# Hybrid decoder block, one core: the seven products of the down-projection in another order

## The chip, the cores and the metric

The kernel runs on one core of one Trainium2 chip. A core has TensorE (PE, with its weight loads shown apart as PEld), VectorE (DVE), ScalarE (ACT), GpSimd (POOL) and SyncE (SP), which issues most transfers. The metric is the device time of one execution in microseconds. The profile shows one further execution: its span runs from the first to the last instruction, and its own time is a little longer than its span.

## The reference

One decoder block over 1024 tokens of width 1024: token mixing (sliding-window attention and an mLSTM), cross-attention into 256 memory tokens, a gated MLP, and a last RMSNorm. The change touches only the end of it:

```
u = hf @ w_up[l]
g = causal_depthwise_conv(u[..., :D_FF], conv_ffn_w[l], conv_ffn_b[l])
x = x + (jax.nn.silu(g) * u[..., D_FF:]) @ w_down[l]
return rmsnorm(x, norm_final_g)
```

Here `D_FF` is 2816, so the down-projection multiplies a 1024 x 2816 matrix by a 2816 x 1024 one, in float32. The result, with the residual added, is normalised row by row and multiplied by the gain `norm_final_g`.

## The kernel before, in words

**Precision.** Every float32 operand is split into a rounded high part (a cast on ACT, tiles `dh`) and a remainder (a subtraction on DVE, tiles `dl`). A product is three matmuls: high x high, high x remainder, remainder x high (`three`, line 139).

**Seven products.** Up- and down-projection are done by a scheme of the Strassen kind: each matrix is cut in 2 x 2 blocks, and seven products of block sums, P1 to P7, replace eight block products. The up-projection (tiles `pu`, `w`, `c`, `fu`, `fa`) writes the left-hand blocks and their sums (`A11`, `A12`, `A22`, `S1` to `S4`) to a scratch tensor `pc_d` in DRAM. The down-projection reads them back. It is what the change is about.

**One step.** The inner dimension is worked through in 11 steps (`kp`, 0 to 10). `step` (line 1162) loads one 128 x 1024 tile `dr` by two transfers of 256 KB on SP's queue: the left half from `pc_d`, the right half from the weights. For P5 and P7 it loads a second weight block (`do`, three buffers) and DVE subtracts it from the right half. For P6 and P4 DVE subtracts with a block kept from an earlier product: P6's sum uses P5's, and P4's uses P6's. P1, P2 and P3 use a plain weight block. I call this subtraction the block difference (`drP<-drP,doP` or `drP<-drP,drP` in the profile). Then ACT casts the tile (`dhP<-drP`) and DVE makes the remainder (`dlP<-drP,dhP`). High parts and remainders live in a ring of six buffers, that is three steps; a cast has to wait until the matmuls of three steps before are done. For the last product they stay in larger buffers for steps 0 to 7, since they are read twice.

**PE.** A step of a product is 12 matmuls of 128 x 512: four blocks of 128 rows (i = 0 to 3, one PSUM bank `pdP` each), three matmuls each. So a product is 132 matmuls. The last product is done in two halves: rows 0 and 1 over all steps (6 matmuls a step), then row 2 over all steps, then row 3, so that rows finish one after the other.

**The order around the change.** The products come P1, P2, P5, P6, P3, P7, P4. What follows a product, adding its four results into the residual rows `x2n` (8 tiles of 128 x 1024, rows 0 to 3 and 4 to 7), is put into a list (`later`) and worked off during the steps of the next product (`work`). A scheduler sets the final order of each engine's instructions in most of this; the part at the end is pinned to the written order. Each engine, and SP's queue, works its instructions off in order.

**The end of a row.** When a half row is done, ACT squares it and sums the squares (`half_done`, line 1227, tiles `sq`, `ms`). For the half that is done first POOL multiplies it by the gain (tile `ot`). When both halves are there, POOL adds the two sums and takes the power -0.5 (`root`, line 1237); I call the chain from the last addition over square, sum and power the root chain. Then (`finish`, line 1242) DVE multiplies the late half by root and gain, ACT scales the early half by the root, and two transfers of 256 KB store the row (line 1250), all on SP's queue but one of the very last row, which ACT issues. Rows 0 to 3 end with P3 (fifth product), rows 4 to 7 with P4 (last).

Of the kernel before, what the change touches and what calls it, by code (L numbers as in the profile page):

```python
# [10 lines left out]
AF = mybir.ActivationFunctionType  # L11
ALU = mybir.AluOpType
# [6 lines left out]
D = 1024  # L19
KT = D // P  # L20
NB = S // P
# [4 lines left out]
EPS = 1e-6  # L26
# [7 lines left out]
NK = NFF // 2  # L34
# [25 lines left out]
def kernel(  # L60
# [5 lines left out]
    nc = tc.nc  # L66
    V, A, G, T = [Pinned(tc, e) for e in (nc.vector, nc.scalar, nc.gpsimd, nc.tensor)]
# [8 lines left out]
    def slot(name, dt=F32, pool=None):  # L76
        return (pool or big).tile([P, SLOT], dt, tag="t", name=name)

    def full(name, dt=F32, pool=None):
        return slot(name, dt, pool)[:, :S]  # L80

    def ps_mm(name):
        return mm.tile([P, HALF], F32, tag="mm", name=name)
# [49 lines left out]
    def w_cols(w, c0, n, k0=0, kn=KT):  # L133

        src = w[k0 * P:(k0 + kn) * P, c0:c0 + n].rearrange("(k p) c -> p k c", p=P)
        hi, lo = load_w([(lambda t: t.rearrange("p (k c) -> p k c", k=kn), src)], kn * n)
        return [t[:, :kn * n].rearrange("p (k c) -> p k c", k=kn) for t in (hi, lo)]
# [188 lines left out]
    with ExitStack() as actx:  # L326
# [75 lines left out]
        for h in range(MH):  # L402
            qk = []
            for s_ in range(2):
# [13 lines left out]
                for d in (1, 2, 3):  # L418
                    V.scalar_tensor_tensor(acc[:, d:], u[:, :S - d], col(C_QK + (3 - d) * 8 + ci), acc[:, d:],
                                           op0=ALU.mult, op1=ALU.add)  # L420
# [3 lines left out]
            if h % 2 == 0:  # L424
# [4 lines left out]
                for which, base in ((0, 1792), (1, 2304)):  # L429
                    if h == 0 and which == 0:  # L430
                        continue
                    parts = [w_cols(win, base + h * P, 2 * P, k0=kk, kn=4) for kk in (0, 4)]
                    for i in range(NB):
                        ps = ps_mm(f"pvo{h}_{which}_{i}")
# [25 lines left out]
            for hf in range(2):  # L460
                psc = ps_sm(f"psc{h}_{hf}")
                for ci in range(4):
# [5 lines left out]
                                       op0=ALU.mult, op1=ALU.mult)  # L468
# [5 lines left out]
                for ci in range(4):  # L474
                    c = hf * 4 + ci
                    A.activation(kt[:, ci * P:(ci + 1) * P], pkt[:, ci * P:(ci + 1) * P], AF.Copy,
                                 scale=W[:, c, P - 1:P])
                pht = ps_sm(f"pht{h}_{hf}")
                for ci in range(4):
# [7 lines left out]
                    if c < NB - 1:  # L487
# [3 lines left out]
                        if c:  # L491
                            V.scalar_tensor_tensor(Cn, C, wbc[:, (c + 1) * P - 1:(c + 1) * P], pu,
                                                   op0=ALU.mult, op1=ALU.add)
# [139 lines left out]
    for i in range(2):  # L633
        t = full(f"mn{i}", pool=ep)
        nc.sync.dma_start(t, mem[0][i * P:(i + 1) * P, :])
        sq = full(f"msq{i}", pool=ep)
# [49 lines left out]
    late = []  # L686
    for ct in range(KT):
# [16 lines left out]
        if ct < 5 or ct == KT - 1:  # L704
            hx += [split_gain(t, f"hx{c}", col(G_X + c)) for c, t in late]
            late = []
# [104 lines left out]
    cp = ctx.enter_context(tc.tile_pool(name="cp", bufs=8, reuse_waits="tile"))  # L811
# [169 lines left out]
    for hf in range(2):  # L981
        sl = slice(hf * HALF, (hf + 1) * HALF)
        sqf = full(f"sqf{hf}")[:, :HALF]
        for k in range(4):
# [4 lines left out]
            for q in range(2):  # L989
# [7 lines left out]
                ps = ps_mm(f"pyx{hf}_{ct}")  # L997
# [149 lines left out]
    xr_ = []  # L1147
# [3 lines left out]
    gfb = full("gfb")  # L1151
    nc.sync.dma_start(gfb, norm_final_g.partition_broadcast(P))
    cols = [slice(0, HALF), slice(HALF, S)]
# [4 lines left out]
    def rows(kp, odd, h):  # L1158
        k = 2 * kp + odd
        return wdn[k * P:(k + 1) * P, cols[h]]  # L1160

    def step(name, piece, kp):

        raw = full(f"dr{name}_{kp}")
        b = raw[:, HALF:S]
        nc.sync.dma_start(raw[:, 0:HALF], pc_d[kp, PIECE[piece]])
        odd, h = {"P1": (0, 0), "P2": (1, 0), "P5": (0, 1), "P6": (1, 1), "P3": (1, 1), "P7": (1, 1), "P4": (1, 0)}[name]
        nc.sync.dma_start(b, rows(kp, odd, h))
        if name in ("P5", "P7"):
            other = wpool.tile([P, WSLOT], F32, tag="raw", name=f"do{name}_{kp}")[:, 0:HALF]  # L1170
            nc.sync.dma_start(other, rows(kp, 0, 1 if name == "P7" else 0))
            V.tensor_tensor(b, b, other, op=ALU.subtract)
        if name == "P6":
            V.tensor_tensor(b, b, kept[kp], op=ALU.subtract)
        if name == "P4":
            V.tensor_tensor(b, kept[kp], b, op=ALU.subtract)
        if name in ("P5", "P6"):
            kept[kp] = b
        ring = not (name == "P4" and kp < NK - 3 or name == "P1" and kp < 3)
        hi, lo = [wpool.tile([P, WSLOT], F32R, tag="ws", name=f"d{q}{name}_{kp}", bufs=6) if ring  # L1180
                  else full(f"d{q}{name}_{kp}", F32R) for q in "hl"]
        A.copy(hi, raw)
        V.tensor_tensor(lo, raw, hi.bitcast(F32), op=ALU.subtract)
        return hi, lo

    def bank(name):
        banks[0] += 1
        return (ps_mm if banks[0] % 8 < 3 else ps_sm)(name)

    def along(ps, i, parts, kp):  # L1190
        hi, lo = parts
        sl = slice(i * P, (i + 1) * P)
        three(ps, hi[:, HALF:S], lo[:, HALF:S], hi[:, sl], lo[:, sl], kp == 0, kp == NK - 1, wstat=False)
# [3 lines left out]
    def work(n):  # L1197

        while todo and n:
            todo.pop(0)()  # L1200
            n -= 1

    def multiply_all(name, piece):
        ps = [bank(f"pd{name}_{i}") for i in range(4)]
        n = -(-len(todo) // (NK - 2))
        for kp in range(NK):
            parts = step(name, piece, kp)
            if name == "P1" and kp == 2:
                ups[-1].end()
            for i in range(4):  # L1210
                along(ps[i], i, parts, kp)
            if kp:
                work(n)
        work(-1)
        return ps

    def later(f, *a):
        todo.append(lambda: f(*a))

    def add(i, h, src, op=ALU.add):  # L1220
        x = xr_[i][:, cols[h]]
        V.tensor_tensor(x, x, src, op=op)


    ots, mss = {}, {}

    def half_done(i, h, early):
        if i not in ots:
            ots[i] = full(f"ot{i}", pool=cp), full(f"sq{i}", pool=cp)
            mss[i] = const.tile([P, 2], F32, name=f"ms{i}", tag="ms", bufs=8)  # L1230
        ot, sq = ots[i]
        A.activation(sq[:, cols[h]], xr_[i][:, cols[h]], AF.Square, scale=D ** -0.5, accum_out=mss[i][:, h:h + 1])
        if early:
            G.tensor_scalar(mss[i][:, h:h + 1], mss[i][:, h:h + 1], EPS, None, op0=ALU.add)
            G.tensor_tensor(ot[:, cols[h]], xr_[i][:, cols[h]], gfb[:, cols[h]], op=ALU.mult)

    def root(i):
        ms = mss[i]
        G.tensor_tensor(ms[:, 0:1], ms[:, 1:2], ms[:, 0:1], op=ALU.add)
        G.tensor_tensor(ms[:, 0:1], ms[:, 0:1], mhalf[:, 0:1], op=ALU.pow)  # L1240

    def finish(i, early):

        ot, r3 = ots[i][0], mss[i][:, 0:1]
        late = 1 - early
        V.scalar_tensor_tensor(ot[:, cols[late]], xr_[i][:, cols[late]], r3, gfb[:, cols[late]],
                               op0=ALU.mult, op1=ALU.mult)
        A.activation(ot[:, cols[early]], ot[:, cols[early]], AF.Copy, scale=r3)
        for h in (late, early):
            (A if h == early and i == NB - 1 else nc.sync).dma_start(  # L1250
                out[0][i * P:(i + 1) * P, cols[h]], ot[:, cols[h]])

    for i, p1 in enumerate(multiply_all("P1", "A11")):
        later(A.copy, U[i], p1)
        later(add, i, 0, p1)
    for i, p2 in enumerate(multiply_all("P2", "A12")):
        later(add, i, 0, p2)
    for i, p5 in enumerate(multiply_all("P5", "S1")):
        later(add, i, 1, p5)
        later(add, 4 + i, 1, p5)  # L1260
    for i, p6 in enumerate(multiply_all("P6", "S2")):
        later(lambda i, p: V.tensor_tensor(U[i], U[i], p, op=ALU.add), i, p6)
        later(add, i, 1, U[i])
    for i in range(4):
        later(add, 4 + i, 1, U[i])
        later(add, 4 + i, 0, U[i])
    for i, p3 in enumerate(multiply_all("P3", "S4")):
        later(add, i, 1, p3)
        later(half_done, i, 0, True)
        later(half_done, i, 1, False)  # L1270
        later(root, i)
        later(finish, i, 0)
    for i, p7 in enumerate(multiply_all("P7", "S3")):
        later(add, 4 + i, 1, p7)
        later(add, 4 + i, 0, p7)
        later(half_done, 4 + i, 1, True)

    parts = []
    ps = [bank(f"pdP4_{i}") for i in range(4)]
    for kp in range(NK):  # L1280
        parts.append(step("P4", "A22", kp))
        for i in range(2):
            along(ps[i], i, parts[kp], kp)
        work(2)
    work(-1)
    Pinned.on = True
    for i in range(4):
        if i > 1:
            for kp in range(NK):
                along(ps[i], i, parts[kp], kp)  # L1290
        add(4 + i, 0, ps[i], ALU.subtract)
        half_done(4 + i, 0, False)
        root(4 + i)
        finish(4 + i, 1)
    Pinned.on = False


# [39 lines left out]
```

## Time and profile before

| | |
|---|---|
| three timed runs, median | 1410.37 us (1408.91 to 1410.59) |
| profiled execution, own time | 1409.79 us |
| its span | 1408.0 us |
| PE, DVE, ACT, POOL busy | 97%, 68%, 43%, 9% of the span |
| mean granted TensorE clock | 0.992 of full speed |
| down-projection, first to last matmul | 1181.08 to 1400.75 us |

In the profile's rows a time is in microseconds from the span's start; a row of the timeline gives start, duration, engine, operation, output and inputs (numbers left out, so that every product's tiles read alike: `pdP`, `dhP`, `dlP`, `drP`), how many it merges, and in brackets how long the engine stood idle before and what ended that. SPq and ACTq are the transfers that SP and ACT issue. PE's duration of one matmul is longer than the distance between two, since they are pipelined.

### The profile page before, as it was taken

The page shows a single profiled execution, that of the slowest core. Times are in us where ns is not written, and L with a number is a line of the kernel's source. Part 1 is how long each engine was busy: PE and PEld are TensorE (multiplying, and loading weights), DVE is VectorE, ACT ScalarE, POOL GpSimd, SP SyncE. Part 2 cuts the span into 40 slices and gives each one's busy share as a digit, 9 for nine tenths or more (in the row PEclk, how much of TensorE's full clock was granted, in tenths as well). Part 3 has the DMA queues.
Part 4 walks back from the last instruction along what each step waited for, and adds up shares of the span by engine and source line. Part 5 has one row for each costly group of instructions (what it writes and reads, how often), then busy time and mean ns, then how long its engine had stood idle before and what let it go on. Part 6 is the DMA issues. An engine that isn't in the chain of part 4 may idle for free.

```text
span 1408.0 us, 18518 instructions
## 1 busy us (share of the span) xinstructions
PE 1371.4 (97%) x6956; PEld 1145.4 (81%) x6956; DVE 963.9 (68%) x1647; ACT 612.1 (43%) x1064; POOL 120.6 (9%) x114
## 2 busy tenths in 40 slices
PE   9999999998999999999998999999999999999997
PEld 8888998776788988888886777888888887888875
DVE  6846616878654634355568888888888886596884
ACT  6264344566643433354443433333333333443453
POOL 0200000001000000000015730000000000020030
PEclk9999999999999999999999999999999999999999
DMA  5321132000244531116350123333333348695751
GB/s 179 94 76 60 31 91 61 22 25 22 92 153 152 178 95 31 30 46 189 111 172 8 30 98 112 112 113 112 99 99 109 113 157 299 234 327 187 232 208 60
DMA packets 168138, 162.59 MB, mean 115 GB/s; under 512 B 16296, under 2 KB 122920, under 8 KB 168048
## 3 DMA queue, kind: packets, MB, share of 16 engines
q1 hardware_dynamic: 166096, 155.03, 33.7%
q10 hardware_dynamic: 1440, 4.54, 0.9%
q0 software_dynamic: 512, 1.84, 0.3%
q8 instruction: 55, 0.90, 0.3%
q14 instruction: 35, 0.29, 0.1%
HBM read 128.57 MB, written 32.80 MB: 115 GB/s over the span
## 4 chain that ended last, share of the span: by engine, by line
PE 81%; DVE 10%; DMA 3%; POOL 2%; issue 2%; ACT 2%; SPq 0%; POOLq 0%; DVEq 0%; ACTq 0%
PE pu_T L50 12%; PE pdP L50 11%; PE pu_B L50 9%; PE pyx L50 6%; PE pmq L50 6%; PE pqx L50 6%; PE py L50 6%; PE pvo L50 4%; PE pvg L50 3%; PE pq L50 2%; PE pkx L50 2%; PE psx L50 2%; PE pox L50 2%; PE pvx L50 2%; PE po L50 2%
## 5 line engine op out<-in xcount | busy, mean ns | idle before, releaser
L50 PE MATMUL pu_T<-T,w_T 128*128 128x512 f32 x1056 | 253.0, 395 | 8.9 <-DVE T L50 2.4
L50 PEld LDWEIGHTS pu_T<-T,w_T 128*128 128x128 f32 x1056 | 200.5, 190 | 55.0 <-DVE T L50 3.4
L50 PE MATMUL pu_B<-B,w_B 128*128 128x512 f32 x792 | 188.7, 392 | 3.3 <-DVE w_B L50 3.0
L50 PEld LDWEIGHTS pu_B<-B,w_B 128*128 128x128 f32 x792 | 149.1, 189 | 35.4 <-DVE w_B L50 3.7
L50 DVE TENSOR_TENSOR wlo<-raw,whi 128x1024 fp32r<-128x1024 f32 x67 | 82.3, 1230 | 91.8 <-ACT whi L50 91.2
L50 PE MATMUL pdP<-dlP,dhP 128*128 128x512 f32 x308 | 121.0, 393 | 5.3 <-DVE dlP L50 5.2
L50 ACT CAST dhP<-drP 128x1024 fp32r<-128x1024 f32 x77 | 80.1, 1052 | 105.4 <-PE pdP L50 73.2
L50 ACT CAST whi<-raw 128x1024 fp32r<-128x1024 f32 x67 | 70.3, 1053 | 122.1 <-PE pqx L50 28.4
L50 DVE TENSOR_TENSOR dlP<-drP,dhP 128x1024 fp32r<-128x1024 f32 x77 | 94.8, 1238 | 37.5 <-ACT dhP L50 35.6
L50 PE MATMUL pdP<-dhP,dlP 128*128 128x512 f32 x308 | 120.0, 390 | 0.0
L50 PE MATMUL pdP<-dhP 128*128 128x512 f32 x308 | 118.4, 391 | 1.6 <-ACT dhP L50 1.6
L50 ACT CAST w_T<-s 128x512 fp32r<-128x512 f32 x66 | 40.6, 621 | 96.1 <-PE pu_T L50 54.5
L50 PEld LDWEIGHTS pdP<-dlP,dhP 128*128 128x128 f32 x308 | 57.8, 188 | 20.9 <-DVE dlP L50 9.3
L50 PEld LDWEIGHTS pdP<-dhP 128*128 128x128 f32 x308 | 57.5, 188 | 14.9 <-ACT dhP L50 3.0
L50 PEld LDWEIGHTS pdP<-dhP,dlP 128*128 128x128 f32 x308 | 57.8, 188 | 11.7
L50 DVE SCALAR_TENSOR_TENSOR fa<-fu,vec,fa 128x1023 f32<-128x1023 f32 (+1 forms) x44 | 58.6, 1331 | 2.7 <-ACT fa L50 2.7
L50 DVE TENSOR_TENSOR c<-pu_T,c 128x512 f32<-128x512 f32 x88 | 58.0, 681 | 0.1
L50 PE MATMUL pvo<-whi,hh 128*128 128x256 f32 x192 | 54.7, 285 | 1.1 <-ACT sg L50 1.1
L50 PE MATMUL pvo<-wlo,hh 128*128 128x256 f32 x192 | 54.4, 283 | 0.0
L50 PE MATMUL pvo<-whi,hl 128*128 128x256 f32 x192 | 54.4, 283 | 0.0
L50 PE MATMUL pmq<-hh,whi 128*128 128x512 f32 x128 | 51.6, 403 | 0.0
L50 PE MATMUL pmq<-hh,wlo 128*128 128x512 f32 x128 | 51.1, 399 | 0.0
(463 smaller groups left out, 3034.9 us busy)
## 6 DMA issues: line engine op xcount, KB each, us to landing
c<-in_w_up_dram SPq DMA_DIRECT2D x44, 512.0 KB, 3.8
drP<-pc_d SPq DMA_DIRECT2D x77, 256.0 KB, 5.1
drP<-in_w_down_dram SPq DMA_DIRECT2D x77, 256.0 KB, 5.2
pc_d<-fa SPq DMA_DIRECT2D x20, 512.0 KB, 3.9
raw<-in_wkv_x_dram SPq DMA_DIRECT2D x16, 512.0 KB, 4.0
raw<-in_wo_x_dram SPq DMA_DIRECT2D x16, 512.0 KB, 3.7
raw<-in_w_in_dram SPq DMA_DIRECT2D x15, 512.0 KB, 3.6
doP<-in_w_down_dram SPq DMA_DIRECT2D x22, 256.0 KB, 4.6
```

The source lines that it names most:

```text
L50: ins = f(*a, **k)
```

## The change

The products come P1, P5, P6, P2, P7, P4, P3. The last one is now P3, whose weight block is plain: its steps have no block difference. Rows 4 to 7 now end with the sixth product (P4), and rows 0 to 3 with the last one (P3). The last product's steps are issued four ahead of their matmuls. The gain of an early half is multiplied on DVE in place (`gained_half`) where POOL did it into a second tile; the tiles `ot` and `sq` go, and the squares are written to one tile `junk`. Rows 4 to 7 are stored from ACT's queue, both halves; rows 0 to 3 as the last rows were before: from SP's queue, but for one half of the last row.

```
-        ring = not (name == "P4" and kp < NK - 3 or name == "P1" and kp < 3)
+        ring = not (name == "P3" and kp < NK - 3 or name == "P1" and kp < 3)
...
-    ots, mss = {}, {}
-
-    def half_done(i, h, early):
-        if i not in ots:
-            ots[i] = full(f"ot{i}", pool=cp), full(f"sq{i}", pool=cp)
+    junk, mss = full("junk", pool=cp), {}
+
+    def half_done(i, h):
+        if i not in mss:
...
-        if early:
-            G.tensor_scalar(mss[i][:, h:h + 1], mss[i][:, h:h + 1], EPS, None, op0=ALU.add)
-            G.tensor_tensor(ot[:, cols[h]], xr_[i][:, cols[h]], gfb[:, cols[h]], op=ALU.mult)
+    def gained_half(i, h):
+
+        G.tensor_scalar(mss[i][:, h:h + 1], mss[i][:, h:h + 1], EPS, None, op0=ALU.add)
+        V.tensor_tensor(xr_[i][:, cols[h]], xr_[i][:, cols[h]], gfb[:, cols[h]], op=ALU.mult)
...
         for h in (late, early):
-            (A if h == early and i == NB - 1 else nc.sync).dma_start(
+            (A if i > 3 or h == early and i == 3 else nc.sync).dma_start(
...
-    for i, p2 in enumerate(multiply_all("P2", "A12")):
-        later(add, i, 0, p2)
     for i, p5 in enumerate(multiply_all("P5", "S1")):
...
-    for i, p3 in enumerate(multiply_all("P3", "S4")):
-        later(add, i, 1, p3)
-        later(half_done, i, 0, True)
-        later(half_done, i, 1, False)
-        later(root, i)
-        later(finish, i, 0)
+    for i, p2 in enumerate(multiply_all("P2", "A12")):
+        later(add, i, 0, p2)
+        later(half_done, i, 0)
+        later(gained_half, i, 0)
     for i, p7 in enumerate(multiply_all("P7", "S3")):
         later(add, 4 + i, 1, p7)
         later(add, 4 + i, 0, p7)
-        later(half_done, 4 + i, 1, True)
+        later(half_done, 4 + i, 1)
+        later(gained_half, 4 + i, 1)
+    for i, p4 in enumerate(multiply_all("P4", "A22")):
+        later(add, 4 + i, 0, p4, ALU.subtract)
+        later(half_done, 4 + i, 0)
+        later(root, 4 + i)
+        later(finish, 4 + i, 1)
...
-    ps = [bank(f"pdP4_{i}") for i in range(4)]
+    ps = [bank(f"pdP3_{i}") for i in range(4)]
     for kp in range(NK):
-        parts.append(step("P4", "A22", kp))
+        while len(parts) < min(kp + 4, NK):
+            parts.append(step("P3", "S4", len(parts)))
         for i in range(2):
             along(ps[i], i, parts[kp], kp)
...
-        add(4 + i, 0, ps[i], ALU.subtract)
-        half_done(4 + i, 0, False)
-        root(4 + i)
-        finish(4 + i, 1)
+        add(i, 1, ps[i])
+        half_done(i, 1)
+        root(i)
+        finish(i, 0)
```

DVE's order in the first half of the last product, before. `P4_5` is step 5 of P4; a tile `dr` on the left of the arrow is a block difference, `dl` a remainder, `x2n7` row 7 of the residual:

```order
L50 TENSOR_TENSOR x2n7_9997<-x2n7_9997,pdP7_3_11166 128x512 x2
L50 TENSOR_TENSOR dlP4_4_11548<-drP4_4_11543,dhP4_4_11547 128x1024
L50 TENSOR_TENSOR drP4_5_11564<-drP6_5_10810,drP4_5_11564 128x512
L50 TENSOR_TENSOR dlP4_5_11569<-drP4_5_11564,dhP4_5_11568 128x1024
L50 TENSOR_TENSOR drP4_6_11585<-drP6_6_10831,drP4_6_11585 128x512
L50 TENSOR_TENSOR dlP4_6_11590<-drP4_6_11585,dhP4_6_11589 128x1024
L50 TENSOR_TENSOR drP4_7_11599<-drP6_7_10852,drP4_7_11599 128x512
L50 TENSOR_TENSOR dlP4_7_11604<-drP4_7_11599,dhP4_7_11603 128x1024
```

DVE's order at the same place, now (the last product is P3, and rows 4 to 7 end here):

```order
L50 TENSOR_TENSOR dlP3_5_11524<-drP3_5_11520,dhP3_5_11523 128x1024
L50 TENSOR_TENSOR x2n4_9991<-x2n4_9991,pdP4_0_11213 128x512
L50 TENSOR_TENSOR x2n5_9993<-x2n5_9993,pdP4_1_11214 128x512
L50 TENSOR_TENSOR x2n6_9995<-x2n6_9995,pdP4_2_11215 128x512
L50 SCALAR_TENSOR_TENSOR x2n4_9991<-x2n4_9991,ms4_11279,gfb_9999 128x512
L50 TENSOR_TENSOR dlP3_6_11539<-drP3_6_11535,dhP3_6_11538 128x1024
L50 TENSOR_TENSOR x2n7_9997<-x2n7_9997,pdP4_3_11216 128x512
L50 SCALAR_TENSOR_TENSOR x2n5_9993<-x2n5_9993,ms5_11325,gfb_9999 128x512
L50 SCALAR_TENSOR_TENSOR x2n6_9995<-x2n6_9995,ms6_11371,gfb_9999 128x512
L50 TENSOR_TENSOR dlP3_7_11558<-drP3_7_11554,dhP3_7_11557 128x1024
L50 SCALAR_TENSOR_TENSOR x2n7_9997<-x2n7_9997,ms7_11417,gfb_9999 128x512
L50 TENSOR_TENSOR dlP3_8_11573<-drP3_8_11569,dhP3_8_11572 128x1024
```

Before, block difference and remainder alternate. Now no block difference stands here; the remainders of steps 0 to 5 stand before the sixth product's results, and those of steps 6 to 8 between the ends of rows 4 to 7.

ACT's order at the same place, before (casts `dh`, squares `sq`):

```order
L50 ACTIVATE sq6_11558,ms6_11559<-x2n6_9995 128x512
L50 CAST dhP4_4_11547<-drP4_4_11543 128x1024
L50 ACTIVATE sq7_11580,ms7_11581<-x2n7_9997 128x512
L50 CAST dhP4_5_11568<-drP4_5_11564 128x1024
L50 CAST dhP4_6_11589<-drP4_6_11585 128x1024
L50 CAST dhP4_7_11603<-drP4_7_11599 128x1024
```

ACT's order at the same place, now:

```order
L50 ACTIVATE junk_10003,ms4_11279<-x2n4_9991 128x512
L50 CAST dhP3_6_11538<-drP3_6_11535 128x1024
L50 ACTIVATE x2n4_9991<-x2n4_9991,ms4_11279 128x512
L50 DMA out_0_dram<-x2n4_9991 128x512 x2
L50 ACTIVATE junk_10003,ms5_11325<-x2n5_9993 128x512
L50 ACTIVATE junk_10003,ms6_11371<-x2n6_9995 128x512
L50 ACTIVATE x2n5_9993<-x2n5_9993,ms5_11325 128x512
L50 DMA out_0_dram<-x2n5_9993 128x512 x2
L50 CAST dhP3_7_11557<-drP3_7_11554 128x1024
L50 ACTIVATE x2n6_9995<-x2n6_9995,ms6_11371 128x512
L50 DMA out_0_dram<-x2n6_9995 128x512 x2
L50 ACTIVATE junk_10003,ms7_11417<-x2n7_9997 128x512
```

After these come the scaling of row 7, the cast of step 8, one store, the cast of step 9, one store and the cast of step 10. So four squares, four scalings and eight stores now stand among the casts of steps 6 to 10.

## Rows read from the trace of the kernel before

**Rows 1.** Page, part 1, busy time of each engine.

```profile
PE 1371.4 (97%) x6956; PEld 1145.4 (81%) x6956; DVE 963.9 (68%) x1647; ACT 612.1 (43%) x1064; POOL 120.6 (9%) x114
```

**Rows 2.** Timeline, PE: first matmuls of products and halves, last matmul.

```profile
1181.08 0.39 PE L50 MATMUL pdP<-dhP 128*128 128x512 f32 x1
...
1212.77 0.39 PE L50 MATMUL pdP<-dhP 128*128 128x512 f32 x1
...
1332.45 0.39 PE L50 MATMUL pdP<-dhP 128*128 128x512 f32 x1
...
1364.96 0.39 PE L50 MATMUL pdP<-dhP 128*128 128x512 f32 x1
...
1386.02 0.39 PE L50 MATMUL pdP<-dhP 128*128 128x512 f32 x1
...
1400.75 0.39 PE L50 MATMUL pdP<-dhP,dlP 128*128 128x512 f32 x1
```

**Rows 3.** Waits of PE from 1330 to 1402 us.

```profile
PE pdP L50 <- DVE dlP L50: 3.8, 7, 0.8
PE pdP L50 <- ACT dhP L50: 1.6, 3, 0.6
```

**Rows 4.** Timeline, DVE and ACT: one step of the last product.

```profile
1372.81 0.68 DVE L50 TENSOR_TENSOR drP<-drP,drP 128x512 f32<-128x512 f32 x1
...
1373.53 1.05 ACT L50 CAST dhP<-drP 128x1024 fp32r<-128x1024 f32 x1 [1.89 <-DVE drP L50]
...
1374.61 1.23 DVE L50 TENSOR_TENSOR dlP<-drP,dhP 128x1024 fp32r<-128x1024 f32 x1 [1.11 <-ACT dhP L50]
...
1375.75 0.68 DVE L50 TENSOR_TENSOR drP<-drP,drP 128x512 f32<-128x512 f32 x1
```

**Rows 5.** Waits of DVE from 1330 to 1402 us, the longest.

```profile
DVE ot L50 <- POOL ms L50: 7.8, 7, 1.8
```

**Rows 6.** Timeline, SP's queue: stores of rows 0 to 3, next load.

```profile
1336.56 10.74 SPq L1250 DMA_DIRECT2D out_dram<-ot  x8
1347.36 0.44 SPq L1166 DMA_DIRECT2D drP<-pc_d  x1
```

**Rows 7.** Timeline: the root chain of the last row.

```profile
1401.17 0.69 DVE L50 TENSOR_TENSOR x2n<-x2n,pdP 128x512 f32<-128x512 f32 x1 [4.35 <-PE pdP L50]
1401.90 0.63 ACT L50 ACTIVATE sq<-x2n 128x512 f32<-128x512 f32 x1 [5.10 <-DVE x2n L50]
...
1402.70 0.19 POOL L50 TENSOR_TENSOR ms<-ms 128x1 f32<-128x1 f32 x1 [6.66 <-ACT sq L50]
...
1403.55 0.72 ACT L50 ACTIVATE ot<-ot,ms 128x512 f32<-128x512 f32 x1 [0.93 <-POOL ms L50]
```

**Rows 8.** Timeline: POOL's gain multiply, and a POOL sum beside DVE.

```profile
1343.82 1.22 DVE L50 TENSOR_TENSOR dlP<-drP,dhP 128x1024 fp32r<-128x1024 f32 x1
...
1344.13 0.95 POOL L50 TENSOR_TENSOR ms<-ms 128x1 f32<-128x1 f32 x1 [3.35 <-ACT sq L50]
...
1363.89 1.29 POOL L50 TENSOR_TENSOR ot<-x2n,gfb 128x512 f32<-128x512 f32 x1 [18.17 <-DVE x2n L50]
```

**Rows 9.** Timeline, ACT: a store that ACT issued in an earlier stage.

```profile
389.28 0.33 ACTq L50 DMA_DIRECT2D x_d<-x  x1
...
389.77 0.52 ACT L50 ACTIVATE hm<-ptm,vec 128x256 fp32r<-128x256 f32 x1
```

**Rows 10.** Stretch of the fifth product (columns: busy us and count, clock, DMA).

```profile
1302.50:1332.40 29.90, 29.90 (x133) 24.77 (x132) 26.25 (x35) 11.61 (x11) 0.00 (x0) 1.00 0.79 252
```

**Rows 11.** Transfers by line: KB each and median us from issue to landing.

```profile
drP<-in_w_down_dram SPq DMA_DIRECT2D x77, 256.0 KB, 5.2
...
doP<-in_w_down_dram SPq DMA_DIRECT2D x22, 256.0 KB, 4.6
...
xin<-in_x_dram SPq DMA_DIRECT2D x7, 512.0 KB, 9.4
...
gfb<-in_norm_final_g_dram SPq DMA_DIRECT2D x1, 512.0 KB, 7.5
```

More of the change, by code (lines that the diff above doesn't have):

```diff
@@ L1222, in add @@
         V.tensor_tensor(x, x, src, op=op)
-    ots, mss = {}, {}
-    def half_done(i, h, early):
-        if i not in ots:
-            ots[i] = full(f"ot{i}", pool=cp), full(f"sq{i}", pool=cp)
+    junk, mss = full("junk", pool=cp), {}
+    def half_done(i, h):
+        if i not in mss:
             mss[i] = const.tile([P, 2], F32, name=f"ms{i}", tag="ms", bufs=8)
-        ot, sq = ots[i]
-        A.activation(sq[:, cols[h]], xr_[i][:, cols[h]], AF.Square, scale=D ** -0.5, accum_out=mss[i][:, h:h + 1])
-        if early:
-            G.tensor_scalar(mss[i][:, h:h + 1], mss[i][:, h:h + 1], EPS, None, op0=ALU.add)
-            G.tensor_tensor(ot[:, cols[h]], xr_[i][:, cols[h]], gfb[:, cols[h]], op=ALU.mult)
+        A.activation(junk[:, cols[h]], xr_[i][:, cols[h]], AF.Square, scale=D ** -0.5, accum_out=mss[i][:, h:h + 1])
+    def gained_half(i, h):
+        G.tensor_scalar(mss[i][:, h:h + 1], mss[i][:, h:h + 1], EPS, None, op0=ALU.add)
+        V.tensor_tensor(xr_[i][:, cols[h]], xr_[i][:, cols[h]], gfb[:, cols[h]], op=ALU.mult)
     def root(i):
@@ L1242, in finish @@
     def finish(i, early):
-        ot, r3 = ots[i][0], mss[i][:, 0:1]
+        ot, r3 = xr_[i], mss[i][:, 0:1]
         late = 1 - early
-        V.scalar_tensor_tensor(ot[:, cols[late]], xr_[i][:, cols[late]], r3, gfb[:, cols[late]],
+        V.scalar_tensor_tensor(ot[:, cols[late]], ot[:, cols[late]], r3, gfb[:, cols[late]],
                                op0=ALU.mult, op1=ALU.mult)
@@ L1263 @@
         later(add, i, 1, U[i])
-    for i in range(4):
         later(add, 4 + i, 1, U[i])
         later(add, 4 + i, 0, U[i])
-    for i, p3 in enumerate(multiply_all("P3", "S4")):
-        later(add, i, 1, p3)
-        later(half_done, i, 0, True)
-        later(half_done, i, 1, False)
-        later(root, i)
-        later(finish, i, 0)
+    for i, p2 in enumerate(multiply_all("P2", "A12")):
+        later(add, i, 0, p2)
+        later(half_done, i, 0)
+        later(gained_half, i, 0)
     for i, p7 in enumerate(multiply_all("P7", "S3")):
```

## The prediction

> **What bounds the kernel now.** I read the busy times first: PE has 97% of the span, no other engine over 68% [rows 1]. So time goes only where PE stands still, or before its first and after its last matmul. Then I took the timeline of PE in the down-projection and compared the starts of the products [rows 2]. From 1212.77 to 1332.45 four products (P2, P5, P6, P3) take 119.68 us, 29.92 each; at 132 matmuls that is 0.2267 us a matmul, and no product of the four differs, so PE waits for nothing there. P1 takes 1212.77 - 1181.08 = 31.69 us, 1.77 more. P7 takes 1364.96 - 1332.45 = 32.51, 2.59 more. The first half of P4, 66 matmuls or 14.96 us, takes 1386.02 - 1364.96 = 21.06, 6.10 more. Its second half, 65 matmuls to the start of the last, takes 14.73 and should take 14.74. So PE loses 10.46 us in the down-projection, 8.69 of it in the last two products. The waits say for what: remainders by DVE, then casts by ACT [rows 3] (the view counts the idle time alone, 5.4 us; the distances above hold the restart too).
>
> The timeline of a step of the last product shows why [rows 4]: block difference on DVE at 1372.81, cast on ACT at 1373.53, remainder on DVE at 1374.61, next block difference at 1375.75. DVE does the next difference only behind this remainder, so the chain is serial, 2.94 us a step, and PE has but 6 x 0.2267 = 1.36 us of work a step there. In P7 the loss is of another kind: DVE stands 7.8 us for POOL's roots between 1330 and 1402 [rows 5], four of these seven waits in P7, where rows 0 to 3 end, and P7's remainders are queued behind them. Also SP's queue holds the eight stores of these rows from 1336.56 to 1347.30, and the last product's loads behind them: the next is issued at 1347.36 [rows 6].
>
> **The change part by part.** All sums are against the profiled execution, 1409.79 us (span 1408.0 and 1.79 around it); the median of the runs is 0.58 above it, and I add that at the end.
>
> *P3 last.* The block difference leaves the serial chain. What is left of a step is one cast (1.05) and one remainder (1.23) on two engines [rows 4], below PE's 1.36 each. Steps 0 to 5 stand in DVE's order before the sixth product's results, so they are ready when the last product begins. The 6.10 goes.
>
> *What is late next.* Rows 4 to 7 now end in this half, and their root chains stand on ACT and DVE among the casts and remainders of steps 6 to 10. I follow the order from T, the last product's first matmul, with durations of rows 4, 7 and 9. The first bank's last matmul starts ten matmuls before T, at T - 2.27; the addition follows 0.42 later (1400.75 to 1401.17) [rows 2, 7], T - 1.85. Square from T - 1.1 to T - 0.3, root ready at T + 0.55 (1402.70 to 1403.55 is 0.85). ACT: cast 6 to T + 0.75, scaling of row 4 (0.72) to 1.45, two stores (0.33 and a gap, say 0.37 each) to 2.2, squares of rows 5 and 6 to 3.8, scaling of row 5 after its root from 3.85 to 4.6, stores to 5.4, cast 7 to 6.45, scaling to 7.2, stores to 7.9, square of row 7 to 8.7, root to 9.55, scaling to 10.25, cast 8 to 11.3; DVE's remainder 8 to 12.5. PE needs step 8 at 8 x 1.36 = T + 10.9. Its high matmuls wait 0.4, the four others until 12.5, so it ends at 13.4 in place of 12.24: 1.2 lost; steps 9 and 10 add 0.1. I take 1.3. Bounds: 0 (if ACT's stores cost it nothing, as at 389.28, where the next instruction starts 0.49 after the store's issue, in the shadow of the one before [rows 9]: 8 x 0.37 = 3.0 us less) and 6.1 (a half as starved as now); 1.3 is nearer the row.
>
> *P7 in fifth place.* The roots leave it, four gain multiplies on DVE come to it. Of the program's order, DVE has 34 instructions there, 12 remainders or as wide and 22 half as wide. The fifth place of before had 35 of these kinds, 26.25 us busy in 29.90, and PE lost nothing [rows 10]. A cast may begin when the step three before is done, 5.44 us ahead; cast and remainder take 2.28; 3.2 are left, of which up to three narrow instructions (0.68 each) take 2.0. So 1.2 us of cover is left, and a transfer that lands 1.2 us late shows. I take a loss of 0.5, between 0 and the 2.59 of now, near the row without loss.
>
> *P5 in second place* loads 33 blocks of 256 KB where P2 loaded 22, and its differences come earlier. Its second blocks have three buffers, so each load waits for the difference three steps back: 4.6 landing [rows 11] and 0.68, 5.3 us for three steps that PE works 8.16 on. I take 0; bounds 0 and 2.59 as P7's now. P6 and P2 move one place each with the same work: 0.
>
> *Eight gain multiplies from POOL to DVE.* 8 x 0.68 = 5.4 us of DVE, four in the fifth product, four in the sixth, where DVE has 15 remainders and 12 narrow instructions, 15 x 1.23 + 12 x 0.68 = 26.6 of 29.92. PE's matmuls hide them. Without that cover each would cost 0.68. POOL's own multiply took 1.29 [rows 8], and off the path.
>
> *Stores from ACT.* SP's queue holds no store before the last product's loads; the 10.74 us [rows 6] that held the loads of steps 1 to 10 back go. What it costs ACT is in the walk. P1 is unchanged, 1.77. The end after the last matmul (1400.75 to 1408.0, 7.25 us) is the same chain and the same queues: 0.
>
> Sum: 1409.79 - 6.10 - 2.59 + 1.3 + 0.5 = 1402.9 in the profiled execution's measure, and with 0.58 more a median of **1403.5 us**.
>
> **The rivals.** *Roots on POOL stretched (B).* POOL's sum over one column took 0.95 us while DVE was in a remainder (1343.82 to 1345.04), and 0.19 with DVE idle [rows 7, 8]. Two POOL operations a row, 0.76 more each: 1.5 a row, 6.1 for four, all on the path of cast 8: up to 1409.6. Against it: in three of the four rows DVE's next instruction waits for that same root, so DVE is idle. With half of it, 3.0, 1406.5. By the Trainium skill (SBUF — State Buffer, Who interferes with whom) a VectorE instruction with two inputs in SBUF and a GpSimd instruction that reads SBUF shut each other out, whichever began second waiting for all of the other. The two sums above agree with that rule. It speaks against this change in one more way: the eight gains are such two-input instructions; by it alone, all four roots would wait, the 6.1.
>
> *A difference ring that shows (C).* P5 or P7 stands as P7 did, 2.59 instead of 0 or 0.5: 1406.1 or 1405.6, both 1408.2. For it: three buffers only, and cover of 1.2 us; against it: rows 10.
>
> *The last half is starved after all (E).* The casts are held by the row ends so long that 6.1 is lost again: 1403.5 + 4.8 = 1408.3. Against it: six steps, 8.2 us, are ready beforehand.
>
> *Slower: loads that land late in front of others (D).* In the new order the casts and remainders of the last product's steps 0 to 3 stand ahead of casts of P7 and P4, and P4's last differences ahead of P7's last remainders, seven places in all. If a load lands late, its whole engine stands. With a landing time L each place costs L - 5.2 - 1.2. It decides from L = 7.8 on, where 7 x 1.4 = 9.7 eats the gain of 6.9 and 2.8 more. Landings of 7.5 and 9.4 are in the trace [rows 11]; at their middle, 8.45, 7 x 2.05 = 14.4: 1417.9. Against it: 5.2 is the median of 77 such loads, in the stretch itself.
>
> **How the numbers follow.** My forecast (1401.7 to 1405.5 for itself) 0.62, B 0.13, C 0.15, E 0.05, D 0.05. Lowest: nothing new is lost, 1410.37 - 8.69 = 1401.7, less 0.5 for the scatter: 1401.2. At the top I go to C with both and stop at 1408.2, which leaves out D, the rest of E and the worst of B: some 0.13 above, 0.04 below. A measurement here tells 0.2% from no change, 2.8 us: 1407.55 to 1413.2 is the same. Faster: 0.62 + 0.10 of B + 0.11 of C + 0.01 of E = 0.84; same: 0.03 of B, 0.04 of C, 0.04 of E = 0.11; slower: D, 0.05.
>
> **What would show it.** In the profile after: the sixth and fifth products 29.9 to 30.5 us from first matmul to first matmul; the last product's first half 15 to 17 us, with any wait of PE in its steps 8 to 10, for a remainder behind a cast that ACT does after row 7's scaling; P1 still at 31.7; 7.25 us from the last matmul to the end. Wrong would be: waits of PE in steps 0 to 5 of the last product or in P4 (then D), a loss in the second product (C), POOL operations of 0.9 us in all four roots (B), or a time that does not move although the last product has no serial chain.

## The result, and the profile after

The changed kernel takes 1402.91 us (median of 5 runs, 1401.81 to 1405.35) where the kernel before took 1410.59 beside it: a ratio of 0.9944 with an interval of 0.9928 to 0.9961. Run again later beside another set of the kernel before, it took 1400.75 against 1408.98, 0.9942 (0.993 to 0.9955). The forecast was 1403.5. The profiled execution took 1401.81 us by itself, its span 1400.0.

Page, part 1, of the kernel after, busy time of each engine; it answers to [rows 1].

```profile
PE 1368.3 (98%) x6956; PEld 1146.5 (82%) x6956; DVE 963.7 (69%) x1655; ACT 611.8 (44%) x1064; POOL 105.0 (7%) x106
```

PE has the same 6956 matmuls. POOL has eight instructions fewer, the gain multiplies, and is 15.6 us less busy. DVE has the eight more, 5.4 us of work, and is not busier. A part of the reason is that POOL's multiplies no longer stretch its other instructions: in e4 and e9 below, with the same 1647 instructions on DVE, it is busy 963.7 us with these multiplies on POOL and 960.6 us without them. What makes up the rest is not shown.

Timeline of PE of the kernel after, as in [rows 2]: first matmul of P1, of the second, sixth and seventh product and of its second half, and the last matmul.

```profile
1179.79 0.39 PE L50 MATMUL pdP<-dhP 128*128 128x512 f32 x1
...
1212.23 0.39 PE L50 MATMUL pdP<-dhP 128*128 128x512 f32 x1
...
1331.91 0.39 PE L50 MATMUL pdP<-dhP 128*128 128x512 f32 x1
...
1361.83 0.39 PE L50 MATMUL pdP<-dhP 128*128 128x512 f32 x1
...
1378.00 0.39 PE L50 MATMUL pdP<-dhP 128*128 128x512 f32 x1
...
1392.73 0.39 PE L50 MATMUL pdP<-dhP,dlP 128*128 128x512 f32 x1
```

From 1212.23 to 1331.91 four products (P5, P6, P2, P7) take 119.68 us, 29.92 each, and the sixth (P4) 29.92 too: five products in which PE waits for nothing. P1 takes 32.44, 2.52 more than 29.92. The last product's first half takes 16.17, 1.21 more than 14.96. The down-projection loses 3.73 us in place of 10.46. The other 1.3 us of the span's 8.0 lie ahead of P1, where both kernels are the same: P1 began at 1179.79 in place of 1181.08, which is scatter (in the runs below it begins anywhere from 1179.5 to 1183.4). From the last matmul to the end 7.27 us pass, as before (7.25).

Waits of PE of the kernel after from 1179 to 1400 us (us in total, times, longest); in [rows 3] two engines held PE in the last 70 us alone.

```profile
PE pdP L50 <- DVE dlP L50: 2.2, 3, 1.4
```

Two of the three waits are P1's. The third is in the last product. Timeline of ACT, DVE and PE of the kernel after there, 9 to 12.5 us behind its first matmul.

```profile
1371.26 0.72 ACT L50 ACTIVATE x2n<-x2n,ms 128x512 f32<-128x512 f32 x1 [0.94 <-POOL ms L50]
1371.89 1.04 ACT L50 CAST dhP<-drP 128x1024 fp32r<-128x1024 f32 x1
...
1372.82 2.00 ACT L50 CAST dhP<-drP 128x1024 fp32r<-128x1024 f32 x2
...
1372.96 3.50 DVE L50 TENSOR_TENSOR dlP<-drP,dhP 128x1024 fp32r<-128x1024 f32 x3 [0.95 <-ACT dhP L50]
...
1374.24 0.50 PE L50 MATMUL pdP<-dlP,dhP 128*128 128x512 f32 x1 [0.53 <-DVE dlP L50]
```

This is the place the forecast named: row 7 is scaled, then cast 8 runs (forecast T + 10.25 to 11.3, it was T + 10.06 to 11.1 with T = 1361.83), then remainder 8, and PE waits for it. Casts 9 and 10 follow cast 8 without a wait. The serial chain of [rows 4] is gone.

Timeline of SP's queue of the kernel after: the loads of the last product's step 8 (second half), step 9 (two halves) and step 10 (two halves). In [rows 6] the queue held stores between the loads of this product.

```profile
1349.55 0.43 SPq L1168 DMA_DIRECT2D drP<-in_w_down_dram  x1
1350.77 0.33 SPq L1166 DMA_DIRECT2D drP<-pc_d  x1
1365.96 0.33 SPq L1168 DMA_DIRECT2D drP<-in_w_down_dram  x1
1369.51 0.33 SPq L1166 DMA_DIRECT2D drP<-pc_d  x1
1370.12 0.33 SPq L1168 DMA_DIRECT2D drP<-in_w_down_dram  x1
```

Nothing of SP stands between them, yet the queue stands still for 15 us between the two halves of step 9. Waits of SP's queue of the kernel after, 1340 to 1390 us.

```profile
SPq L1168 <- DMA out_dram<-x2n: 15.1, 2, 14.8
```

A load of SP waits for a store that ACT issued. That was in no step of the forecast; run e6 takes it up.

### The profile page after: what moved, and what is told of

The parts are those of the page before. It is cut to its first block, busy times and chain, and to the rows that moved or that the text cites. A ratio compares the mean times of both kernels' runs of the same rounds, so it can differ in the third digit from the quotient of the medians.

```text
span 1400.0 us, 18505 instructions
## 1 busy us (share of the span) xinstructions
PE 1368.3 (98%) x6956; PEld 1146.5 (82%) x6956; DVE 963.7 (69%) x1655; ACT 611.8 (44%) x1064; POOL 105.0 (7%) x106
## 4 chain that ended last, share of the span: by engine, by line
PE 84%; DVE 9%; POOL 2%; issue 2%; ACT 1%; DMA 1%; ACTq 0%; POOLq 0%; SPq 0%; DVEq 0%
PE pdP L50 13%; PE pu_T L50 13%; PE pu_B L50 10%; PE pyx L50 6%; PE pqx L50 6%; PE py L50 6%; PE pmq L50 6%; PE pvo L50 4%; PE pvg L50 3%; PE pq L50 2%; PE pkx L50 2%; PE psx L50 2%; PE pox L50 2%; PE pvx L50 2%; PE po L50 2%
## 5 line engine op out<-in xcount | busy, mean ns | idle before, releaser
L50 PE MATMUL pu_T<-T,w_T 128*128 128x512 f32 x1056 | 253.5, 396 | 10.2 <-DVE c L50 3.5
L50 PEld LDWEIGHTS pdP<-dhP 128*128 128x128 f32 x308 | 57.7, 188 | 12.9 <-ACT dhP L50 0.9
```

Source lines behind the costliest of these rows:

```text
L50: ins = f(*a, **k)
```

## The experiments

My theory after the result: S, the serial chain of the last product (block difference, cast, remainder) was the 6.10 us, and its end is the gain. The rival L: the last product's loads were late, since they stood behind eight stores in SP's queue. Every run has its profile, and from PE's starts each place's loss in us: its length less 29.92 (14.96 for a half). What is not listed lost nothing; a ratio is to the kernel before in the same set of runs.

| run | P1 | fifth | sixth | last, first half | median us | ratio and interval |
|---|---|---|---|---|---|---|
| before | 1.77 | 0 | 2.59 (P7) | 6.10 | 1410.59 | |
| after | 2.52 | 0 (P7) | 0 | 1.21 | 1402.91 | 0.9944 (0.9928 to 0.9961) |
| e1 before, no difference | 1.50 | 0 | 0.71 (P7) | 0 | 1403.55 | 0.9952 (0.9937 to 0.9966) |
| e2 before, stores on ACT | 1.96 | 0 | 1.35 (P7) | 8.82 | 1412.35 | 1.0015 (1.0006 to 1.0024) |
| e3 order alone | 1.59 | 1.88 (P7) | 0 | 5.88 | 1408.69 | 0.9986 (0.9976 to 0.9997) |
| e4 after, gains on POOL | 1.95 | 2.06 (P7) | 0 | 0 | 1403.29 | 0.995 (0.9933 to 0.9966) |
| e5 after, stores on SP | 1.98 | 0 | 0 | 7.15 | 1406.99 | 0.9985 (0.9976 to 0.9994) |
| e6 after, stores on POOL | 2.06 | 0 | 0 | 0.42 | 1402.5 | 0.9945 (0.993 to 0.996) |
| e7 early loads | 0.48 | 0 | 0 | 1.19 | 1401.32 | 0.9939 (0.9926 to 0.9951) |
| e8 early loads, six ahead | 0.22 | 0 | 0 | 0.02 | 1399.92 | 0.9927 (0.9915 to 0.994) |
| e9 after, no gains | 1.73 | 0 | 0 | 0 | 1400.81 | 0.994 (0.9927 to 0.9954) |
| e10 after, not ahead | 3.17 | 0 | 0 | 2.56 | 1402.84 | 0.9952 (0.9937 to 0.9967) |
| e11 after again | 1.88 | 0 | 0 | 1.18 | 1400.75 | 0.9942 (0.993 to 0.9955) |

Sets of runs differ by up to 2 us in the kernel before itself (1408.98 to 1410.84), so medians of different sets are compared by their ratios, and single us are read from the losses.

**e1, the chain alone.** In the kernel before:

```diff
-        if name == "P4":
-            V.tensor_tensor(b, kept[kp], b, op=ALU.subtract)
```

> The kernel before, with one thing left out: P4, still the last product, multiplies the plain weight block, its block difference on DVE is not computed. Theory S (the serial chain difference, cast, remainder starves the last product): the first half of the last product falls from 21.06 us to 15 to 16.5, P7 keeps its 32.5, the median falls by 4.6 to 6.1 us, to 1404.5 to 1406. Rival L (its loads are late, because they stand behind eight stores in SP's queue): the half stays at 19 us or more and the median within 2 us of the kernel before.

Timeline of PE of e1: first matmul of the last product and of its second half.

```profile
1365.09 0.39 PE L50 MATMUL pdP<-dhP 128*128 128x512 f32 x1
...
1380.05 0.39 PE L50 MATMUL pdP<-dhP 128*128 128x512 f32 x1
```

The half takes 14.96 us in place of 21.06, its matmuls alone, with all eight stores still ahead of the loads of steps 3 to 10 in SP's queue: S, not L. The median falls by 7.3 (1410.84 beside it), more than expected, since P7 falls too, from 2.59 to 0.71, where S had it unchanged: P4's differences stand on DVE among P7's remainders, and with them gone the same roots cost P7 little. The run also frees DVE of 11 x 0.68 us and buffers earlier (the loads of steps 0 to 2 leave before the stores), so it shows what the difference costs with all that hangs on it. That no load is late in the kernel before is read from its own trace: in the first half of the last product no cast and no instruction of DVE waits for a transfer. Waits of ACT of the kernel before, 1364.96 to 1386 us, the longest in total.

```profile
ACT dhP L50 <- DVE drP L50: 7.7, 5, 1.9
```

**e2, the stores alone.** In the kernel before:

```diff
-            (A if h == early and i == NB - 1 else nc.sync).dma_start(
+            (A if i < 4 or h == early and i == NB - 1 else nc.sync).dma_start(
```

> The kernel before, with the stores of rows 0 to 3 issued by ACT in place of SP, nothing else. Theory S: the last product's first half stays at 20.5 to 21.1 us, since its chain is on DVE and ACT; P7 stays at 32 to 33.5 us, since its remainders are queued behind scalings that wait for POOL's roots; the median stays within 1.5 us of the kernel before. Rival L: the loads of the last product come 10.7 us earlier and the half falls below 18 us, the median by 3 us or more.

The half does not shrink. It grows, to 23.78 us, which S did not expect either. PE's waits begin a step earlier, at step 4: on DVE the eight additions of P7's results now stand ahead of the difference of step 4, where six stood, and it runs at T + 4.1 in place of T + 1.8 (T: first matmul of the last product). By itself this run does not decide against L, since the loads did not come 10.7 us earlier. Those of steps 1 to 4 left 12.9, 5.0, 4.7 and 2.2 us earlier, those of steps 5 to 10 within 2.4 us of the kernel before: SP's loads now waited for stores that ACT issued (e6 takes that up). Waits of SP's queue of e2, 1340 to 1390 us.

```profile
SPq L1166 <- DMA out_dram<-ot: 12.2, 3, 8.1
```

L falls by e1 and by the trace of the kernel before. P7 loses 1.35 in place of 2.59, so a part of that loss went with the stores; the median is 1.5 us worse all the same.

**e3 and e4, the order without its companions.** e4 is the changed kernel with the first of these edits, e3 with both:

```diff
-        V.tensor_tensor(xr_[i][:, cols[h]], xr_[i][:, cols[h]], gfb[:, cols[h]], op=ALU.mult)
+        G.tensor_tensor(xr_[i][:, cols[h]], xr_[i][:, cols[h]], gfb[:, cols[h]], op=ALU.mult)
...
-            (A if i > 3 or h == early and i == 3 else nc.sync).dma_start(
+            (A if h == early and i == 3 else nc.sync).dma_start(
```

> The changed kernel with the eight gain multiplies back on POOL and the stores of rows 4 to 7 back on SP; the new order of the products and the steps issued four ahead stay. Theory S: the order carries the gain. DVE has 8 x 0.68 us less to do and PE does not notice; the loads of steps 8 to 10 stand behind the stores of rows 4 to 6 in SP's queue, and the last half loses 1.2 to 2.5 us; median 1402 to 1404.5. Rival G (the moves of gain and stores carry a part of it): the fifth product or the last half loses 2.6 us more than in the changed kernel, median 1405.5 or more.

> The changed kernel with the eight gain multiplies back on POOL, the stores of rows 4 to 7 still from ACT. Theory S: no product changes; on ACT the casts of steps 7 and 8 now stand before the scalings of rows 5 and 6, so the last half loses 0 to 1 us in place of 1.2; median 1401.5 to 1403.5. Rival B (POOL multiplies of two SBUF inputs and DVE's remainders hold one another up): products four and five lose 1 us or more each, median 1404.5 or more.

The order alone is worth 1 us of the 6.7 (losses 9.4 in place of 10.46): G holds, and my theory missed the median by 4 us. Its last half loses 5.88 and P7, in the fifth place and without a root in it, 1.88. With the stores on ACT (e4) the half loses nothing, P7 still 2.06: of rival B's two products one loses, and the median lies in the range of S, whose "no product changes" failed. Timeline of DVE and POOL of e4 in P7.

```profile
1309.25 1.29 POOL L50 TENSOR_TENSOR x2n<-x2n,gfb 128x512 f32<-128x512 f32 x1
1309.62 1.47 DVE L50 TENSOR_TENSOR drP<-drP,doP 128x512 f32<-128x512 f32 x1
...
1311.23 1.60 POOL L50 TENSOR_TENSOR x2n<-x2n,gfb 128x512 f32<-128x512 f32 x1
1311.61 2.30 DVE L50 TENSOR_TENSOR dlP<-drP,dhP 128x1024 fp32r<-128x1024 f32 x1
...
1313.84 2.98 DVE L50 TENSOR_TENSOR drP<-drP,drP 128x512 f32<-128x512 f32 x3
1314.06 1.60 POOL L50 TENSOR_TENSOR x2n<-x2n,gfb 128x512 f32<-128x512 f32 x1
```

A difference that takes 0.68 elsewhere takes 1.47, a remainder 2.30 in place of 1.22, each beside a gain multiply of POOL. PE then waits 1.4 us for remainders (twice, 1.0 at the longest). That points to POOL as the cause, but DVE's order in e4 also differs from that of the changed kernel; e9 parts the two.

**e9, no gains.** In the changed kernel:

```diff
-        V.tensor_tensor(xr_[i][:, cols[h]], xr_[i][:, cols[h]], gfb[:, cols[h]], op=ALU.mult)
```

> The changed kernel with the eight gain multiplies left out, so that rows miss the gain in half of their columns. DVE's order is that of the run with the gains on POOL, but for two instructions. Theory X (in that run the fifth product lost 2.06 us because POOL's multiplies of two SBUF inputs stretched DVE's differences and remainders): the fifth product loses 0 to 0.3 us, its remainders take 1.22 us throughout, median 1400.5 to 1402.5. Rival (the order of DVE's instructions is what loses it): the fifth product loses 1.5 us or more, median 1402.6 or more.

The fifth product loses nothing. Timeline of DVE and POOL of e9 at the same place.

```profile
1306.33 5.05 POOL L50 TENSOR_SCALAR ms<-ms 128x1 f32<-128x1 f32 x1 [1.14 <-ACT junk L50]
...
1306.56 1.22 DVE L50 TENSOR_TENSOR dlP<-drP,dhP 128x1024 fp32r<-128x1024 f32 x1
1307.69 1.89 DVE L50 TENSOR_TENSOR drP<-drP,drP 128x512 f32<-128x512 f32 x3
```

The same three differences take 1.89 in place of 2.98, the remainder 1.22 in place of 2.30, in the same order. So it was POOL's multiplies: X holds, the rival falls. By the Trainium skill (SBUF — State Buffer, Who interferes with whom) a VectorE instruction with two inputs in SBUF and a GpSimd instruction that reads SBUF exclude each other, and the order of issue decides who waits. The trace agrees in both directions: DVE's instructions are longer here in e4, POOL's one-column addition in e9 (5.05 us).

**e5, the stores alone, after.** In the changed kernel the second edit of e3 alone.

> The changed kernel with the stores of rows 4 to 7 back on SP, nothing else. In SP's queue all eight stand before the loads of step 8. Theory Q (a store that waits at the head of SP's queue holds the loads behind it): ACT is spared 8 store issues, row 7 is scaled at about T + 8, the load of step 8 is issued at T + 9.5 to 10, lands 5.2 later, and with cast and remainder step 8 is ready at T + 17, where PE wants it at T + 10.9 (T: first matmul of the last product): the last half loses 5.5 to 6.5 us, median 1407 to 1408.5. Rival (the loads are hidden anyway): the last half loses at most 1.2, median at most 1403.

Q holds: 7.15 us lost, 5.94 more than after, with the median (1406.99) at the low end of its range. Timeline of SP's queue of e5 in the last product (T = 1361.03), and the cast of step 8 on ACT.

```profile
1362.44 3.39 SPq L1250 DMA_DIRECT2D out_dram<-x2n  x4
1365.88 0.44 SPq L1168 DMA_DIRECT2D drP<-in_w_down_dram  x1
1366.41 2.91 SPq L1250 DMA_DIRECT2D out_dram<-x2n  x4
1369.37 0.45 SPq L1166 DMA_DIRECT2D drP<-pc_d  x1
...
1375.43 1.04 ACT L50 CAST dhP<-drP 128x1024 fp32r<-128x1024 f32 x1 [5.05 <-DMA drP<-in_w_down_dram]
```

The stores wait for their rows, the loads of steps 8 to 10 wait behind them until T + 8.3, and ACT stands 5.05 us for step 8. My 5.5 to 6.5 was too low by what the next view shows: windows of e5 (columns: us; busy us and count of PE, weight loads, DVE, ACT, POOL; granted clock; DMA share; GB/s).

```profile
1372.73:1376.53 3.80, 0.40 (x2) 0.00 (x1) 0.02 (x1) 1.04 (x1) 0.00 (x0) 0.71 0.88 292
1376.53:1381.50 4.97, 4.93 (x11) 3.50 (x12) 3.65 (x3) 2.09 (x2) 0.00 (x0) 0.53 0.05 17
1381.50:1386.00 4.50, 4.50 (x21) 3.70 (x20) 1.44 (x3) 1.45 (x3) 0.74 (x2) 1.00 0.00 0
```

Behind 3.40 us without a matmul the granted clock is 0.53 over 5 us, near the lower of its two levels (1.2 GHz), and then 1.00 again (2.4 GHz). Seven matmuls from 1377.79 take 3.15 us where 7 x 0.2267 is 1.59: 1.6 us of the loss are the clock's. In the kernel after it is 1.00 through the whole product.

**e6, who holds the loads.** In the changed kernel:

```diff
-            (A if i > 3 or h == early and i == 3 else nc.sync).dma_start(
+            (G if i > 3 else A if h == early and i == 3 else nc.sync).dma_start(
```

> The changed kernel with the stores of rows 4 to 7 issued by POOL in place of ACT. In the trace of the changed kernel the load of step 8's second half is issued 15 us after its first half and the wait is put down to a store from ACT. Theory M (loads from SP and stores from ACT take turns on the same eight completion semaphores, so a load waits until a store that took its semaphore has landed): SP's loads of steps 8 to 10 are all issued before the first matmul of the last product. Rival (they wait for their buffers): they are issued where they were, at T + 4 to T + 8.3. By both the last half loses 0.8 to 1.6, since the casts stand behind row 7's root, which now waits behind POOL's store issues of 0.6 to 1 us each; median 1402 to 1404.

M holds. (The load that this expectation calls step 8's is step 9's, counted from the end of the queue.) Timeline of SP's queue of e6: step 10's two loads, and what comes next; and ACT's casts 8 to 10.

```profile
1356.00 0.33 SPq L1166 DMA_DIRECT2D drP<-pc_d  x1
1356.37 0.43 SPq L1168 DMA_DIRECT2D drP<-in_w_down_dram  x1
...
1373.62 2.93 ACT L50 CAST dhP<-drP 128x1024 fp32r<-128x1024 f32 x3
...
1382.62 15.81 SPq L1250 DMA_DIRECT2D out_dram<-x2n  x7
```

All loads are out 8 us before T (1364.34), while in the kernel after those of steps 9 and 10 left up to 8.3 us behind it. So the buffers were free: it was the stores from ACT that held SP's loads. The half loses 0.42, less than I expected for both: ACT is free of eight issues, and POOL's issues took 0.55 to 0.6 us each, not up to 1. Cast 8 starts at T + 9.28 in place of T + 10.06, 0.78 earlier, and the half loses 0.79 less.

**e10, not ahead.** In the changed kernel:

```diff
-        while len(parts) < min(kp + 4, NK):
+        while len(parts) < min(kp + 1, NK):
```

> The changed kernel with the steps of the last product issued one at a time in place of four ahead. ACT's order then has cast 7 behind row 7's square and cast 8 behind the stores of row 7. Theory W (casts behind row ends set the last half): step 7's remainder ends at T + 9.9 and PE wants it at T + 9.5, step 8's at T + 12.6 and PE wants it at T + 10.9; the last half loses 1.3 to 2 us in place of 1.2, median 1402.5 to 1404. Rival A (issuing ahead is what frees the last product): it loses 4 us or more, median 1405.5 or more.

W holds in part. The price was 2.56 where I had 1.3 to 2: by the distances of PE's matmuls 1.4 us are lost at steps 7 and 8, as forecast, and 1.2 at step 10, whose cast waited 1.92 us for its load. Cast 7 runs at T + 7.5 in place of T + 5.7, cast 8 at T + 10.2, nearly where it was. Issuing ahead is worth some 1.4 us of the half.

**e7 and e8, what the losses that are left point to.** P1's three first remainders stand on DVE in the chain that ends the up-projection, since their loads come behind eight row loads and the gain. e7 moves these loads; e8 adds the second edit.

```diff
-        nc.sync.dma_start(xr_[i], x2_d[i * P:(i + 1) * P, :])
...
+            if name == "P1" and kp > 2:
+                late_load(kp - 3)
...
-        while len(parts) < min(kp + 4, NK):
+        while len(parts) < min(kp + 6, NK):
```

> The changed kernel, with the eight row loads and the gain's load (5 MB ahead of P1's loads in SP's queue) moved to P1's steps 3 to 10. Theory H (P1 loses 2.5 us because the remainders of its steps 0 to 2 land in the last up-projection's chain on DVE, after loads that came late behind the row loads): the first five remainders of P1 are done before that chain, P1 loses 0 to 0.6, median 1400.3 to 1401.2. Rival (the chain on DVE alone sets it, or the row loads then collide with P1's weights): P1 or the second product loses 2 us or more, median 1402.5 or more.

> The kernel of the run before, with the steps of the last product issued six ahead in place of four. On ACT cast 7 stands before the stores of row 5, cast 8 before row 7's square, cast 9 before its scaling. Theory W (the last half's 1.2 us is cast 8 behind row 7's end): it loses 0 to 0.4, median 1399.2 to 1400.4. Rival (cast 8 to 10 wait for loads that were held until stores from ACT had landed): it loses 1 us or more, as before.

The first cast of P1, timeline of ACT, of the kernel after:

```profile
1173.55 1.05 ACT L50 CAST dhP<-drP 128x1024 fp32r<-128x1024 f32 x1 [8.78 <-DMA drP<-in_w_down_dram]
```

and of e7:

```profile
1144.28 1.05 ACT L50 CAST dhP<-drP 128x1024 fp32r<-128x1024 f32 x1
```

It comes 29 us earlier, and P1 loses 0.48. H holds. (The median, 1401.32, is 0.1 above the stretch I gave.) In e8 the last half loses 0.02; timeline of ACT of e8 there: cast 8, row 7's square, cast 9, row 7's scaling.

```profile
1366.40 1.05 ACT L50 CAST dhP<-drP 128x1024 fp32r<-128x1024 f32 x1 [0.61 <-ACT x2n L50]
1367.36 0.63 ACT L50 ACTIVATE junk<-x2n 128x512 f32<-128x512 f32 x1
...
1367.98 1.04 ACT L50 CAST dhP<-drP 128x1024 fp32r<-128x1024 f32 x1
1369.42 0.72 ACT L50 ACTIVATE x2n<-x2n,ms 128x512 f32<-128x512 f32 x1 [0.40 <-POOL ms L50]
```

W holds there too: with the casts ahead of row 7's end the half loses nothing. e8 is the fastest of all: 1399.92, 0.9927 of the kernel before. Its interval and that of the changed kernel overlap, so the times alone do not part the two; the losses do, 0.24 in place of 3.73 or 3.06.

**e11, the changed kernel again.**

> The changed kernel itself. P1 lost 2.52 us in its first profile and 1.5 to 2.1 in six other kernels that are the same up to there. Theory (scatter in when the row loads land): P1 loses 1.5 to 2.1 here, the last half 1.2, the products between 0, median 1401.8 to 1403.5. Rival (the change lengthens P1): P1 loses 2.4 or more again.

P1 loses 1.88, the half 1.18: scatter, as expected. Over the eleven profiles without e7's edit P1 loses 1.50 to 3.17. The median, 1400.75, is 1 us below what I gave; the kernel before beside it, 1408.98, is the lowest of all sets too.

## Why the prediction was right, point by point

The total was right, and so were the place and size of what is left: by the forecast's terms the down-projection still loses 3.57 us (10.46 - 6.10 - 2.59 + 1.3 + 0.5), and it lost 3.73 and 3.06 in the two profiles. But two of its terms were put down to the wrong part of the change, in opposite ways, and made up for each other. This did not hurt, since the change makes both moves; priced in the same way, the order without its companions came out 4 us wrong (e3).

- *P3 last: the 6.10 goes.* The cause was right (e1: without the difference the half loses nothing). But in the new order the step by itself gives back 0.2 (e3, 5.88 lost): the chain goes, and the loads behind the stores take its place.
- *Stores from ACT.* I named the queue, and priced the removal at nothing but ACT's issues in the walk. That is the term that was sized wrongly: it is worth 5.9 (e3 to e4, 5.88 to 0; e5 to after, 7.15 to 1.21). Only in the new order: in the old one the last store leaves SP's queue 17 us before the last product begins (1347.36 and 1364.96), and moving the stores costs (e2). The two terms were 6.1 together, and what I charged to one needs both.
- *P7 in fifth place, 0.5.* It loses nothing. The reason I gave, that the roots leave it, was a misreading in part. With the roots in place but without P4's differences among its remainders it lost 0.71 in place of 2.59 (e1), and of the 7.8 us of [rows 5] only 2.6 lie in P7. Nor is it enough that the roots leave: with the gains on POOL it loses 1.88 to 2.06 there without a root.
- *Eight gain multiplies, 0.* They are worth 2 us in P7, because POOL no longer holds DVE up, and the order on ACT that comes with them costs 1.2 in the last half (e4 and e9 lose 0 there). Net some 0.8. The rule of rival B was right; I turned it against the change, where it speaks for it.
- *Last half, 1.3.* It lost 1.21 and 1.18, with the wait at remainder 8. That cast 8 behind row 7's end is the cause is shown by moving it: at T + 10.06 the half loses 1.21, at T + 9.28 (e6) 0.42, ahead of row 7's scaling (e8, and in e4 too) nothing. e10, with cast 7 later and cast 8 where it was, adds loss at step 7, and at step 10 by a late load.
- *P5 0, tail 0, P1 unchanged.* The first two as forecast. P1 lost 2.52 and 1.88 in two profiles of the same kernel, 1.77 before: within its scatter.
- *Rival B.* Of the last half's four roots one was stretched, beside DVE's scaling of row 5; in the others DVE waited for the root, as I had argued against this rival. Timeline of POOL of the kernel after, rows 5 and 6:

```profile
1364.93 0.19 POOL L50 TENSOR_TENSOR ms<-ms 128x1 f32<-128x1 f32 x1 [2.50 <-ACT junk L50]
1365.20 0.56 POOL L50 TENSOR_TENSOR ms<-ms,mhalf 128x1 f32<-128x1 f32 x1
1365.73 0.20 POOL L50 TENSOR_TENSOR ms<-ms 128x1 f32<-128x1 f32 x1
1366.01 0.95 POOL L50 TENSOR_TENSOR ms<-ms,mhalf 128x1 f32<-128x1 f32 x1
```

- *Rivals C, E, D.* C and D did not come. E, a last half as starved as before, did not come either, but it lay one queue away: e3 and e5 are that case, by late loads and not by casts.

## What to carry to other kernels

An order of work and the queues that its stores stand in are one change: move the order, and ask for each store that now falls into the last stage which loads are queued behind it. An instruction that is hidden on a slack engine may still hold up another one, so a multiply on an idle POOL can cost more than on a busy DVE (here 2.06 us of P7 for four of them). A stage's loss is read best as its length less its matmuls times their pitch; it tells tenths of a us where the whole time scatters by two.

## What the hardware showed that I had not expected

- A load waits for another engine's store. In the program the loads that SP issues and the stores that ACT issues take turns on eight completion semaphores, and an issue waits until the transfer that used its semaphore last has landed. In the records of the kernel after, the load issued at 1365.96 has the semaphore of ACT's store of 1363.64, which landed at 1365.95; in e6 POOL's stores have semaphores that SP's loads do not use. It held SP 14.8 us in one piece in the kernel after and 0 with the stores on POOL (e6). In the kernel after it cost nothing that shows: the loads that were held are those of steps 9 and 10, and casts 9 and 10 follow cast 8 without a wait. In e10 it did, at step 10.
- A POOL instruction on one column took 5.05 us beside a run of DVE instructions with two inputs (e9, 1306.33 to 1311.38; DVE's run ended at 1311.31), against 0.38 for the same form 4 us before. By these times it waited for several of them, not for one.
- A wait of 3.40 us of PE cost 1.6 us more in the clock behind it (e5), and one of 2.27 us in e3 as much (granted clock 0.67 from 1380.28 to 1385.50); after the waits of the kernel after, the longest 1.4 us, it stayed at 1.00.
